# A batched transposed matmul: fixed instruction order, stores on ScalarE's queue, the last four stores held back

## Chip, cores, metric

One core of a Trainium2 chip. The time is the device time of a run in microseconds (us); the span is the time from the first to the last instruction of the profiled run, some 1.8 us shorter. A run of one core has no second die to compare with, so a run counts as fast when it lies within 1.5% of the fastest of its kernel; ratios and profiles below are of fast runs. Batches are numbered 0 to 15.

## The reference

```python
# a: (16, 512, 512) = batch, k, m      b: (16, 512, 512) = batch, n, k      both float32
def reference(a, b):
    return np.matmul(a.transpose(0, 2, 1), b.transpose(0, 2, 1)).astype(np.float32)
```

Each batch reads 1 MB of a and 1 MB of b and writes 1 MB: 48 transfers of 1 MB in all.

## The kernel before

Per batch, VectorE casts b to bf16 (`bc`), TensorE transposes it (eight 128x128 blocks, two bf16 in each float32), VectorE copies the transposes to SBUF, ScalarE casts a, TensorE does sixteen matmuls into four PSUM tiles, and ScalarE and VectorE evict two of these each.

```python
LAG = 3
def load(i):                       # b_sb, a_sb: 4 buffers each
    nc.sync.dma_start(b_sb, b_v[i]);  nc.sync.dma_start(a_sb, a_v[i])

def prepare(i):
    nc.vector.tensor_copy(bc, b_sb)
    for j in range(KJ):
        for no in range(NO):
            nc.tensor.transpose(bt_ps[:, no, :], bc_w[:, no, j, :], identity)
        nc.vector.tensor_copy(bt_w[:, j, :, :], ...)        # cut
    for h in range(2):
        nc.scalar.copy(a_bf[...], a_sb[...])                # cut

def multiply(i):
    for rm in range(MO):           # four matmuls into o_ps, then
        if rm % 2 == 0: nc.scalar.copy(o_sb[:, rm, :], o_ps)
        else:           nc.vector.tensor_copy(o_sb[:, rm, :], o_ps)

for i in range(B + 1):             # the scheduler may reorder this
    if i < B:          load(i); prepare(i)
    if i >= 1:         multiply(i - 1)
    if i >= LAG + 1:   nc.sync.dma_start(out_v[i - 1 - LAG], o_tiles.pop(i - 1 - LAG))
for j in range(B - LAG, B):        # last three stores
    nc.sync.dma_start(out_v[j], o_tiles.pop(j))
```

Of the kernel before, what the change touches and what calls it, by code (L numbers as in the profile page):

```python
# [1 line left out]

# [5 lines left out]


@with_exitstack
def kernel(
    ctx: ExitStack,
    tc: tile.TileContext,
    a: bass.AP,
    b: bass.AP,
    out: bass.AP,
):
    nc = tc.nc
    P = 128  # L20
    B, K, M = a.shape
    _, N, _ = b.shape
    KO = K // P
    KJ = KO // 2
    MO = M // P
    NO = N // P

    f32 = mybir.dt.float32
    cdt = mybir.dt.bfloat16



    a_v = a.rearrange("b (ki ko) m -> b ki ko m", ko=KO)
    b_v = b.rearrange("b (ni no) k -> b ni no k", no=NO)
    out_v = out.rearrange("b (mi mo) n -> b mi mo n", mo=MO)

    const = ctx.enter_context(tc.tile_pool(name="const", bufs=1))
    identity = const.tile([P, P], f32)
    make_identity(nc, identity)

    a_pool = ctx.enter_context(tc.tile_pool(name="a_pool", bufs=4))
    b_pool = ctx.enter_context(tc.tile_pool(name="b_pool", bufs=4))
    ac_pool = ctx.enter_context(tc.tile_pool(name="ac_pool", bufs=3))
    bc_pool = ctx.enter_context(tc.tile_pool(name="bc_pool", bufs=2))
    bt_pool = ctx.enter_context(tc.tile_pool(name="bt_pool", bufs=3))
    o_pool = ctx.enter_context(tc.tile_pool(name="o_pool", bufs=6))
    psum_t = ctx.enter_context(tc.tile_pool(name="psum_t", bufs=4, space=bass.MemoryType.PSUM))
    psum_o = ctx.enter_context(tc.tile_pool(name="psum_o", bufs=4, space=bass.MemoryType.PSUM))

    LAG = 3  # L50
    o_tiles, a_tiles, b_tiles, a_use, b_use = {}, {}, {}, {}, {}

    def load(i):
        b_tiles[i] = b_sb = b_pool.tile([P, NO, K], f32, name="b_sb")
        nc.sync.dma_start(b_sb, b_v[i])  # L55
        a_tiles[i] = a_sb = a_pool.tile([P, KO, M], f32, name="a_sb")
        nc.sync.dma_start(a_sb, a_v[i])  # L57

    def prepare(i):
        b_sb, a_sb = b_tiles.pop(i), a_tiles.pop(i)  # L60



        bc = bc_pool.tile([P, NO, K], cdt, name="bc")
        nc.vector.tensor_copy(bc, b_sb)  # L65
        bc_w = bc.bitcast(f32).rearrange("p no (pk j) -> p no j pk", j=KJ)
        bt_sb = bt_pool.tile([P, KJ, N], f32, name="bt_sb")


        bt_w = bt_sb.rearrange("p j (ni no) -> p j ni no", no=NO)  # L70
        for j in range(KJ):
            bt_ps = psum_t.tile([P, NO, P], f32, name="bt_ps")
            for no in range(NO):
                nc.tensor.transpose(bt_ps[:, no, :], bc_w[:, no, j, :], identity)  # L74
            nc.vector.tensor_copy(bt_w[:, j, :, :], bt_ps.rearrange("p no ni -> p ni no"))  # L75
        b_use[i] = bt_sb.bitcast(cdt).rearrange("p j (n h) -> p j h n", h=2)

        a_bf = ac_pool.tile([P, KO, M], cdt, name="a_bf")
        for h in range(2):
            nc.scalar.copy(a_bf[:, 2 * h:2 * h + 2, :], a_sb[:, 2 * h:2 * h + 2, :])  # L80
        a_use[i] = a_bf.rearrange("p rk (pm rm) -> p rk rm pm", rm=MO)

    def multiply(i):
        a_br, bt_h = a_use.pop(i), b_use.pop(i)
        o_tiles[i] = o_sb = o_pool.tile([P, MO, N], f32, name="o_sb")
        for rm in range(MO):
            o_ps = psum_o.tile([P, N], f32, name="o_ps")
            for rk in range(KO):
                nc.tensor.matmul(  # L89
                    o_ps,  # L90
                    a_br[:, rk, rm, :],
                    bt_h[:, rk // 2, rk % 2, :],
                    start=(rk == 0),
                    stop=(rk == KO - 1),
                )
            if rm % 2 == 0:
                nc.scalar.copy(o_sb[:, rm, :], o_ps)  # L97
            else:
                nc.vector.tensor_copy(o_sb[:, rm, :], o_ps)  # L99



    for i in range(B + 1):
        if i < B:
            load(i)
            prepare(i)
        if i >= 1:
            multiply(i - 1)
        if i >= LAG + 1:
            nc.sync.dma_start(out_v[i - 1 - LAG], o_tiles.pop(i - 1 - LAG))  # L110
    for j in range(B - LAG, B):
        nc.sync.dma_start(out_v[j], o_tiles.pop(j))


# [1 line left out]
_INS = ['a', 'b']  # L116
_OUTS = [((16, 512, 512), 'float32')]


# [23 lines left out]
```

## Time and profile before

| | before |
|---|---|
| median of the first four runs | 128.36 us (127.01 to 128.58) |
| span of the profiled run | 125.4 us |
| DMA engines busy with the kernel's own transfers | 96% of the span |
| TensorE matmul, VectorE, ScalarE busy | 68%, 49%, 41% |

The prediction below reads the rest of this page. The one part that it doesn't show matters later: the list of DMA issues, whose last column is the median time from issue to landing, in us.

```profile
b_sb<-in_b_dram SPq DMA_DIRECT2D x16, 1024.0 KB, 19.6
a_sb<-in_a_dram SPq DMA_DIRECT2D x16, 1024.0 KB, 19.6
out_dram<-o_sb SPq DMA_DIRECT2D x16, 1024.0 KB, 19.6
```

All 48 transfers stand in one queue, so a store waits its turn behind the loads issued before it: 19.6 us is eight transfers of 2.46 us (1 MB at the 427 GB/s of the full slices).

### The profile page before, as it was taken

To read this page: it belongs to the slowest core of one execution; us is meant where nothing else is said; L and a number is where in the kernel's file an instruction comes from. 1 tells how busy PE (TensorE), PEld (TensorE's weight loads), DVE (VectorE), ACT (ScalarE), POOL (GpSimd) and SP (SyncE) were. 2 spreads that over 40 slices of the span, in tenths; PEclk is the share of its full clock that TensorE was granted. 3 is DMA by queue.
4 is the path that set the end of the run, shared out by engine and by line. 5 is a ranking of instruction groups with operands and counts; after the bars stand their busy time and mean duration, and the time that the engine had idled before them with its cause. 6 is when DMAs were issued, how large, how long until landed. Compare 5 with 4: busy or idle time off the path is not lost.

```text
span 125.4 us, 1110 instructions
## 1 busy us (share of the span) xinstructions
PE 85.0 (68%) x384; PEld 45.8 (36%) x384; DVE 60.9 (49%) x80; ACT 51.3 (41%) x65; POOL 0.7 (1%) x6
## 2 busy tenths in 40 slices
PE   0069799999637939396694874939489395693920
PEld 0055356655232334152431534424153152433400
DVE  0255758686452274646607447254742546627420
ACT  4044556846305361533618063361701708154210
POOL 2000000000000000000000000000000000000000
PEclk9999999999995899999859999999976999999996
DMA  3999999999999999999999999999999999999835
GB/s 94 426 431 423 426 423 426 418 350 421 413 428 431 423 426 426 434 428 421 423 431 431 423 415 428 434 423 418 426 436 423 423 423 431 428 418 426 371 154 219
DMA packets 6918, 50.41 MB, mean 402 GB/s; under 512 B 768, under 2 KB 768, under 8 KB 768
## 3 DMA queue, kind: packets, MB, share of 16 engines
q1 hardware_dynamic: 6912, 50.33, 96.1%
q8 instruction: 3, 0.05, 0.2%
q14 instruction: 3, 0.02, 0.0%
HBM read 33.55 MB, written 16.78 MB: 401 GB/s over the span
## 4 chain that ended last, share of the span: by engine, by line
PE 47%; DMA 22%; DVE 17%; issue 7%; ACT 2%; SPq 1%; ACTq 0%
PE o_ps L89 41%; DMA a_sb<-in_a_dram 22%; DVE bc L65 10%; PE bt_ps L74 7%; DVE bt_sb L75 6%; ACT a_bf L80 2%; DVE o_sb L99 1%; SPq L55 1%; SPq L110 0%; ACTq L80 0%; SPq L57 0%
## 5 line engine op out<-in xcount | busy, mean ns | idle before, releaser
L89 PE MATMUL o_ps<-bt_sb,a_bf 128*128 128x512 bf16 x256 | 66.7, 414 | 5.1 <-DVE bt_sb L75 3.0
L89 PEld LDWEIGHTS <-a_bf 128*128 128x128 bf16 x256 | 29.6, 117 | 38.1 <-issue 12.5
L99 DVE COPY o_sb<-o_ps 128x512 f32<-128x512 f32 x32 | 22.1, 691 | 37.8 <-PE o_ps L89 17.0
L97 ACT COPY o_sb<-o_ps 128x512 f32<-128x512 f32 x32 | 18.8, 587 | 52.6 <-PE o_ps L89 52.6
L74 PE MATMUL bt_ps<-identity,bc 128*128 128x128 f32 x128 | 19.6, 298 | 29.9 <-DVE bc L65 29.9
L80 ACT CAST a_bf<-a_sb 128x1024 bf16<-128x1024 f32 x32 | 31.9, 1045 | 15.0 <-DMA a_sb<-in_a_dram 14.7
L74 PEld LDWEIGHTS bt_ps<-identity,bc 128*128 128x128 f32 x128 | 17.4, 209 | 35.6 <-issue 35.0
L75 DVE COPY bt_sb<-bt_ps 128x512 f32<-128x512 f32 x32 | 20.7, 686 | 14.6 <-PE bt_ps L74 14.6
L65 DVE CAST bc<-b_sb 128x2048 bf16<-128x2048 f32 x16 | 19.5, 1220 | 7.4 <-DMA b_sb<-in_b_dram 7.4
L80 ACT ACT_TABLE_LOAD x1 | 1.3, 1283 | 0.7 <-PEq L127 0.7
masks.py:199 POOL TENSOR_SCALAR_AFFINE_SELECT identity<-identity 128x128 f32<-128x128 f32 x1 | 0.3, 295 | 0.1
masks.py:197 POOL MEMSET identity<- 128x128 f32 x1 | 0.2, 205 | 0.3 <-POOLq L127 0.3
L127 POOL MEMSET const-bfloat16-1.0<- 128x1 bf16 x1 | 0.1, 102 | 0.0
L127 POOL MEMSET const-uint8-127<- 128x1 uint8 x1 | 0.1, 102 | 0.0
L127 POOL MEMSET const-float32-0.0<- 128x1 f32 x1 | 0.1, 99 | 0.2 <-issue 0.2
L127 POOL MEMSET const-float32-1.0<- 128x1 f32 x1 | 0.1, 99 | 0.0
## 6 DMA issues: line engine op xcount, KB each, us to landing
b_sb<-in_b_dram SPq DMA_DIRECT2D x16, 1024.0 KB, 19.6
a_sb<-in_a_dram SPq DMA_DIRECT2D x16, 1024.0 KB, 19.6
out_dram<-o_sb SPq DMA_DIRECT2D x16, 1024.0 KB, 19.6
```

The source lines that it names most:

```text
L55: nc.sync.dma_start(b_sb, b_v[i])
L65: nc.vector.tensor_copy(bc, b_sb)
L74: nc.tensor.transpose(bt_ps[:, no, :], bc_w[:, no, j, :], identity)
L75: nc.vector.tensor_copy(bt_w[:, j, :, :], bt_ps.rearrange("p no ni -> p ni no"))
L80: nc.scalar.copy(a_bf[:, 2 * h:2 * h + 2, :], a_sb[:, 2 * h:2 * h + 2, :])
L89: nc.tensor.matmul(o_ps, a_br[:, rk, rm, :], bt_h[:, rk // 2, rk % 2, :], start=(rk == 0), stop=(rk == KO - 1),)
L97: nc.scalar.copy(o_sb[:, rm, :], o_ps)
L99: nc.vector.tensor_copy(o_sb[:, rm, :], o_ps)
L127: nc = _bacc.Bacc("TRN2", target_bir_lowering=False, num_devices=1)
```

## The change

Its intent: let no scheduler reorder the engines; transpose b of the next batch ahead of the matmuls of this one; give the stores a queue of their own; and near the end keep the DMA engines for the last loads, so that the four stores held back fill the time of the last batches' compute.

```diff
-    LAG = 3
+    DEPTH = 4
+    HELD = 4
+    def store(i):
+        nc.scalar.dma_start(out_v[i], o_tiles.pop(i))
     # prepare(i) is split into turn_b(i) and cast_a(i); turn_b does all 8 transposes
     # into one tile of two PSUM banks (2 buffers instead of 4), then both copies     (cut)
-    for i in range(B + 1): ...                                                      (cut)
+    with tc.manual_schedule():
+        for i in range(DEPTH):
+            load(i)
+        turn_b(0)
+        cast_a(0)
+        for i in range(B):
+            if i + 1 < B:
+                turn_b(i + 1)
+            multiply(i)
+            if i + 1 < B:
+                cast_a(i + 1)
+            if i < B - HELD:
+                store(i)
+            elif i + 2 >= B:
+                for j in range(B - HELD if i + 2 == B else i, i + 1):
+                    store(j)
+            if i + DEPTH < B:
+                load(i + DEPTH)
```

More of the change, by code (lines that the diff above doesn't have):

```diff
@@ L46 @@
     o_pool = ctx.enter_context(tc.tile_pool(name="o_pool", bufs=6))
-    psum_t = ctx.enter_context(tc.tile_pool(name="psum_t", bufs=4, space=bass.MemoryType.PSUM))
+    psum_t = ctx.enter_context(tc.tile_pool(name="psum_t", bufs=2, space=bass.MemoryType.PSUM))
     psum_o = ctx.enter_context(tc.tile_pool(name="psum_o", bufs=4, space=bass.MemoryType.PSUM))
-    LAG = 3
+    DEPTH = 4
+    HELD = 4
     o_tiles, a_tiles, b_tiles, a_use, b_use = {}, {}, {}, {}, {}
@@ L57, in load, with turn_b @@
         nc.sync.dma_start(a_sb, a_v[i])
-    def prepare(i):
-        b_sb, a_sb = b_tiles.pop(i), a_tiles.pop(i)
+    def store(i):
+        nc.scalar.dma_start(out_v[i], o_tiles.pop(i))
+    def turn_b(i):
+        b_sb = b_tiles.pop(i)
         bc = bc_pool.tile([P, NO, K], cdt, name="bc")
@@ L67, in prepare, with cast_a @@
         bt_sb = bt_pool.tile([P, KJ, N], f32, name="bt_sb")
-        bt_w = bt_sb.rearrange("p j (ni no) -> p j ni no", no=NO)
+        bt_ps = psum_t.tile([P, KJ, NO, P], f32, name="bt_ps")
         for j in range(KJ):
-            bt_ps = psum_t.tile([P, NO, P], f32, name="bt_ps")
             for no in range(NO):
-                nc.tensor.transpose(bt_ps[:, no, :], bc_w[:, no, j, :], identity)
-            nc.vector.tensor_copy(bt_w[:, j, :, :], bt_ps.rearrange("p no ni -> p ni no"))
+                nc.tensor.transpose(bt_ps[:, j, no, :], bc_w[:, no, j, :], identity)
+        for j in range(KJ):
+            nc.vector.tensor_copy(
+                bt_sb[:, j, :].rearrange("p (ni no) -> p ni no", no=NO),
+                bt_ps[:, j, :, :].rearrange("p no ni -> p ni no"),
+            )
         b_use[i] = bt_sb.bitcast(cdt).rearrange("p j (n h) -> p j h n", h=2)
+    def cast_a(i):
+        a_sb = a_tiles.pop(i)
         a_bf = ac_pool.tile([P, KO, M], cdt, name="a_bf")
@@ L99, in multiply @@
                 nc.vector.tensor_copy(o_sb[:, rm, :], o_ps)
-    for i in range(B + 1):
-        if i < B:
+    with tc.manual_schedule():
+        for i in range(DEPTH):
             load(i)
-            prepare(i)
-        if i >= 1:
-            multiply(i - 1)
-        if i >= LAG + 1:
-            nc.sync.dma_start(out_v[i - 1 - LAG], o_tiles.pop(i - 1 - LAG))
-    for j in range(B - LAG, B):
-        nc.sync.dma_start(out_v[j], o_tiles.pop(j))
+        turn_b(0)
[13 more added lines that the diff above has]
+                load(i + DEPTH)
 _INS = ['a', 'b']
```

## The prediction

> **What bounds the kernel now.** I read the page's DMA rows first, because 50.33 MB in 125.4 us leaves little room.
>
> ```profile
> PEclk9999999999995899999859999999976999999996
> DMA  3999999999999999999999999999999999999835
> GB/s 94 426 431 423 426 423 426 418 350 421 413 428 431 423 426 426 434 428 421 423 431 431 423 415 428 434 423 418 426 436 423 423 423 431 428 418 426 371 154 219
> q1 hardware_dynamic: 6912, 50.33, 96.1%
> ```
>
> Each slice is 3.135 us. The middle slices hold about 427 GB/s, so 1 MB (1,048,576 bytes) takes 2.46 us and the 48 transfers need 118 us. The rest of the span is lost in few places: the first slice (2.4 us), the dip in slice 9 (0.6 us), and the last three slices, which miss 56, 273 and 208 GB/s of 427, together 3.9 us. A better order can win part of those 3.9 us and hardly anything else.
>
> Second, the chain of waits in order of time, because a full DMA row doesn't say that the DMA ends last.
>
> ```profile
> 105.41 0.04 DVE o_sb L99
> 105.44 0.57 issue
> 106.02 1.23 DVE bc L65
> 107.24 0.14 issue
> 107.38 0.73 PE bt_ps L74 x4
> ...
> 108.13 0.70 DVE bt_sb L75
> 108.84 0.04 issue
> 108.88 3.81 PE o_ps L89 x16
> ```
>
> From 43 us to the end the chain contains no DMA at all. It is one ring: the last eviction of batch i on VectorE, the cast of b of the next batch behind it, transposes, their copy, sixteen matmuls. It takes 7.30 us a batch, beside 3 x 2.46 = 7.37 us of DMA. So two bounds lie on top of each other, and the ring decides when the last output exists. The timeline shows the ring's gaps on TensorE:
>
> ```profile
> 107.38 1.20 PE L74 MATMUL bt_ps<-identity,bc 128*128 128x128 f32 x8 [2.01 <-DVE bc L65]
> 108.88 3.79 PE L89 MATMUL o_ps<-bt_sb,a_bf 128*128 128x512 bf16 x16 [0.30 <-DVE bt_sb L75]
> 111.80 0.59 ACT L97 COPY o_sb<-o_ps 128x512 f32<-128x512 f32 x1 [0.55 <-PE o_ps L89]
> 112.28 2.00 ACT L80 CAST a_bf<-a_sb 128x1024 bf16<-128x1024 f32 x2
> ```
>
> 2.01 + 1.20 + 0.30 + 3.79 = 7.30. The last matmuls start at 116.18 and end at 119.98; the last store is issued at 120.76 and takes 3.9 us to land (the shortest landing of the output's DMAs), which gives 124.7 and the span of 125.4 with 0.7 us after it. The last loads were issued at 89.02 and 91.54 and took about 19.6 us, so they were in by 109 and 111: the last batch waited for the ring, not for its data.
>
> **What the Trainium skill says.** "DMA: Bandwidth & Descriptors", section "Issuing engines are not separate DMA queues": transfers started by different engines run on the same 16 DMA engines; only issue time is saved. The trace agrees as far as it goes: 427 GB/s come from one queue with all engines full, so a second queue has nothing to add. The same page, "Queues, rings and completion order", says that an engine serves the queue rows with work in turn, packet by packet. So stores on ScalarE's queue would pass the waiting loads at half the rate, without changing the sum; only one queue is used before, so this isn't shown. "TensorE: Matmul & The Clock Gate", its table at the top, calls ScalarE and VectorE strict FIFO. The trace agrees: each cast of b starts 0.61 us after the eviction ahead of it, at 106.02 after 105.41, though its data is long in. The same page's Part 1 gives half clock after an idle window of about 3.4 us. Here the clock falls with gaps of 3.5 us between the real matmuls (three times, batch 61.87 takes 5.38 us instead of 3.79), so 1.6 us each.
>
> **The change part by part.**
>
> Order. The new text puts turn_b(i+1) ahead of multiply(i) and, with the order fixed, so do the engines. On VectorE: cast b(i+1), two copies, two evictions of batch i, cast b(i+2). On TensorE: transposes(i+1), matmuls(i), transposes(i+2). The copies now lie under matmuls, so the 0.30 goes. But cast b(i+2) still stands behind the last eviction of batch i, so the 2.01 stays, and the 1.20 stays. The ring is 2.01 + 1.20 + 3.79 = 7.00 us, a gain of 0.30 a batch or 4.5 us in 15. ScalarE's ring (eviction, two casts of 1.0 us) is shorter and doesn't count.
>
> Start. Batch 0's matmuls started at 9.19 before; now they wait for the transposes of batch 1. Its b landed at 10.58; cast 1.23, gap 0.14, transposes at half clock 1.96 (as the first ones were): 13.9. Sixteen matmuls, the first four of them at half clock (0.43 against 0.237 us, my guess of the count): 18.5. Then batch i's matmuls start at 18.5 + 2.01 + 1.20 + 7.00 (i-1), batch 14's at 112.7. The start gives back what the ring wins.
>
> Do the loads keep up? In flight or queued are at most the four loads of each input, as before; each batch frees 7.37 us of DMA work per 7.00 us, so the DMA never runs dry before the loads end. b of batch 14 has 29 loads and 12 stores up to it: 3.1 + 41 x 2.46 = 104.0, so its matmuls of batch 13 can't start before 106.6, where the ring says 105.7. That costs up to 0.9 us. The last load lands at 3.1 + 44 x 2.46 = 111.3, as early as before. I take batch 14 at 113.6, and with a mean of a bit over half a clock drop (below) 114.5.
>
> Hold. Stores 12 to 14 stand on ScalarE behind its last eviction of batch 14 and the casts of a(15). From the start of batch 14's matmuls: third group 2.92 (116.18 to 119.10 before), eviction 0.48, casts 2.00: issued at +5.4, so 119.9. Between 111.3 and about 120.5 the DMA has nothing to do: 9 us, where the kernel before lost 3.9. Batch 15's matmuls start after the first half of the cast, +4.5, end at +8.3, its last store is issued at +9.1, while the three ahead occupy the DMA until +13.5, so it queues. End: 5.4 + 0.1 + 1.44 (landing 3.9 less 2.46) + 4 x 2.46 + 0.7 = 17.5 after 114.5, a span of 132.0. The run of the profile took 127.22 for a span of 125.4, so 1.8 on top: **133.8 us**.
>
> In short: ring -4.5, later start and colder clock +4.4, DMA limit +0.9, and after the last matmuls 3 more stores than before. From the end of batch 15's matmuls to the end of the span it is now 17.5 - 8.3 = 9.2 us instead of 5.4: +3.8. The rest is clock drops and the ScalarE cast that delays batch 15.
>
> **Rivals.**
>
> First, the intent: the holding clears the way for the last loads, and four stores fill the DMA while the last batches compute. Then there would be 118 us of transfers, 3.1 ahead and 1.5 behind: a span near 122.6, some 124.4 us. For it speaks the DMA row. Against it: the loads aren't what the last batches wait for, and the stores wait for ScalarE's work after the loads, not only for the loads.
>
> Second, the hold costs, but the DMA idles less: if the early ring ran as fast as batches 1 to 4 do before (4.85 us apart, where the cast of b stood ahead of the evictions), batch 14 would be bound by its load at 111.1 and the end be 128.6, or 130.4 us. The fixed order forbids that on VectorE.
>
> Third, the clock. The gap between real matmuls falls from 3.50 to 3.21 us. If only gaps over the window drop the clock, no drop is left and the time is about 132.9; if it goes on as before, two or three drops make 136 to 138.
>
> Fourth, loads and stores interleaved by packet could move less than 427 GB/s; 2% less would be 2 us more, which adds to a ring that waits for loads.
>
> **Range and chances.** The centre is 133.8, 4% above the median of 128.47 and 5% above the profiled run's 127.22. Downward the ring sets a floor: 112.7 without drops and waits gives 132.0, and a warmer start or one cast fewer on the path gives some 130.5. Upward two more drops and a slower DMA give 137.5. Faster by over 2% needs the first rival: 4%. Within 2% (125.9 to 131.0) needs the second, or a start warmer than I think: 9%. Slower: 87%.
>
> **What would show it.** A DMA row with two to three nearly empty slices after 111 us, then full slices to the end; TensorE's wait for the cast of b still 2.0 us a batch but no wait for the copy; matmul starts 7.0 us apart; the three stores issued on ScalarE's queue right behind the last casts near 120; the last load landed near 111. I am wrong if the last casts on ScalarE end before 113, if the DMA row stays full to the end, or if the ring is shorter than 6.7 us.

## The result

| | before | after |
|---|---|---|
| median | 128.36 us | 132.19 us (131.66 to 134.0, the last a slow run) |
| ratio | | 1.0308 (95% interval 1.0207 to 1.0408) |
| span of the profiled run | 125.4 us | 130.8 us |
| mean granted clock | 0.951 | 0.961 |

Slower by 3.1%. A ratio is the mean time of one kernel's fast runs over that of the other's of the same rounds, so not quite the ratio of the medians.

The page of the changed kernel, the rows in 40 slices of 3.27 us (clock, DMA, GB/s), then the two DMA queues (q1 SyncE's, q10 ScalarE's) and the stores' time to landing:

```profile
PEclk9999999999999995999999999977999999999995
DMA  3999999999999999999999999999999999104995
GB/s 125 426 424 434 419 426 328 408 426 426 431 418 429 429 426 426 429 426 429 426 426 431 424 429 424 419 431 421 426 431 424 426 434 419 58 5 200 431 411 241
q1 hardware_dynamic: 4608, 33.56, 61.6%
q10 hardware_dynamic: 2304, 16.78, 30.6%
...
out_dram<-o_sb ACTq DMA_DIRECT2D x16, 1024.0 KB, 9.0
```

Three slices near the end (58, 5 and 200 GB/s) miss 369, 422 and 227 of 427, together 7.8 us of empty DMA. And a store now lands 9.0 us after its issue instead of 19.6: it passes loads that were issued earlier (store 0, issued at 18.78 us, landed at 28.85; b of batch 5, issued at 15.56, at 36.04).

The end in the timeline (start, duration, engine; in brackets the idle time before and what ended it):

```profile
114.44 1.19 PE L75 MATMUL bt_ps<-identity,bc 128*128 128x128 f32 x8 [2.01 <-DVE bc L69]
115.47 3.79 PE L98 MATMUL o_ps<-bt_sb,a_bf 128*128 128x512 bf16 x15
...
118.39 0.58 ACT L106 COPY o_sb<-o_ps 128x512 f32<-128x512 f32 x1 [1.23 <-PE o_ps L98]
118.57 0.34 ACTq L61 DMA_DIRECT2D out_dram<-o_sb  x1
118.87 1.05 ACT L89 CAST a_bf<-a_sb 128x1024 bf16<-128x1024 f32 x1
119.03 0.37 ACTq L61 DMA_DIRECT2D out_dram<-o_sb  x1
...
119.97 0.64 PE L98 MATMUL o_ps<-bt_sb,a_bf 128*128 128x512 bf16 x2 [0.71 <-ACT a_bf L89]
120.07 0.34 ACTq L61 DMA_DIRECT2D out_dram<-o_sb  x1
120.91 2.88 PEld L98 LDWEIGHTS <-a_bf 128*128 128x128 bf16 x14 [0.80 <-ACT a_bf L89]
...
125.09 0.34 ACTq L61 DMA_DIRECT2D out_dram<-o_sb  x1
```

The ring is there (2.01 us of waiting for the cast of b, no wait for the copy) and takes 6.84 us (107.59, the transposes before, to 114.44). The held stores go out at 118.57, 119.03 and 120.07. The first is issued 0.3 us before the first of the two casts ahead of it in ScalarE's program begins.

In the middle two matmul groups run at half clock, and two transposes wait much longer than the ring's 2.01 us (3.44 and 2.84). TensorE's timeline:

```profile
47.39 1.19 PE L75 MATMUL bt_ps<-identity,bc 128*128 128x128 f32 x8 [2.07 <-DVE bc L69]
48.42 5.40 PE L98 MATMUL o_ps<-bt_sb,a_bf 128*128 128x512 bf16 x15
...
77.78 1.20 PE L75 MATMUL bt_ps<-identity,bc 128*128 128x128 f32 x8 [3.44 <-DVE bc L69]
78.81 3.80 PE L98 MATMUL o_ps<-bt_sb,a_bf 128*128 128x512 bf16 x16
85.45 1.27 PE L75 MATMUL bt_ps<-identity,bc 128*128 128x128 f32 x8 [2.84 <-DVE bc L69]
86.94 4.95 PE L98 MATMUL o_ps<-bt_sb,a_bf 128*128 128x512 bf16 x15 [0.23 <-issue]
```

### The profile page after: what moved, and what is told of

The parts are those of the page before. It is cut to its first block, busy times and chain, and to the rows that moved or that the text cites. A ratio compares the mean times of both kernels' runs of the same rounds, so it can differ in the third digit from the quotient of the medians.

```text
span 130.8 us, 1093 instructions
## 1 busy us (share of the span) xinstructions
PE 82.2 (63%) x377; PEld 46.0 (35%) x384; DVE 61.3 (47%) x80; ACT 50.4 (39%) x65; POOL 0.7 (1%) x6
## 4 chain that ended last, share of the span: by engine, by line
PE 45%; DMA 29%; DVE 12%; issue 6%; ACT 2%; SPq 1%; ACTq 1%; DVEq 0%
PE o_ps L98 34%; DMA b_sb<-in_b_dram 22%; PE bt_ps L75 11%; DVE bc L69 10%; DMA out_dram<-o_sb 7%; ACT a_bf L89 2%; DVE o_sb L108 1%; ACTq L61 1%; ACT o_sb L106 0%; SPq L58 0%; SPq L56 0%; DVEq L69 0%
## 5 line engine op out<-in xcount | busy, mean ns | idle before, releaser
L98 PE MATMUL o_ps<-bt_sb,a_bf 128*128 128x512 bf16 x249 | 63.7, 405 | 1.6 <-ACT a_bf L89 1.0
L75 PE MATMUL bt_ps<-identity,bc 128*128 128x128 f32 x128 | 20.8, 310 | 40.5 <-DVE bc L69 40.5
```

Source lines behind the costliest of these rows:

```text
L75: nc.tensor.transpose(bt_ps[:, j, no, :], bc_w[:, no, j, :], identity)
L98: nc.tensor.matmul(o_ps, a_br[:, rk, rm, :], bt_h[:, rk // 2, rk % 2, :], start=(rk == 0), stop=(rk == KO - 1),)
```

## The experiments

First theories. A: the ring ends late and the hold adds little. B: the hold is the main cost, as the prediction's +3.8 us says. Medians, with the kernel before of the same job:

| run | what differs | median us | before us | ratio (95%) |
|---|---|---|---|---|
| no_hold | nothing held | 132.32 | 128.49 | 1.0312 (1.024 to 1.039) |
| stores_sp | all stores on SyncE's queue | 130.02 | 128.49 | 1.0123 (1.006 to 1.019) |
| tail_sp | last four stores on SyncE's queue | 132.76 | 128.49 | 1.0310 (1.022 to 1.040) |
| cast_early | next cast of b ahead of the evictions | 131.04 | 128.49 | 1.0220 (1.013 to 1.031) |
| order_alone | the order only; stores SyncE, 3 behind | 127.13 | 128.06 | 0.9963 (0.992 to 1.000) |
| before_stores_act | before, stores on ScalarE's queue | 130.38 | 128.06 | 1.0249 (1.017 to 1.033) |
| own_early | transposes(i) before matmuls(i) | 131.78 | 128.06 | 1.0314 (1.020 to 1.043) |
| own_early_sp | own_early, stores SyncE | 127.45 | 128.06 | 0.9952 (0.992 to 0.999) |
| order_lag_act | order_alone, stores on ScalarE's queue | 132.72 | 128.25 | 1.0355 (1.030 to 1.041) |
| order_nolag | order_alone, stores not behind | 128.71 | 128.25 | 1.0037 (0.999 to 1.009) |
| own_early_lag | own_early_sp, stores 3 behind | 126.46 | 128.25 | 0.9865 (0.982 to 0.991) |
| lag_act_tail_sp | order_lag_act, late stores SyncE | 126.94 | 127.67 | 0.9948 (0.992 to 0.997) |

All gave correct results. Measured against a line of 2%, no_hold, tail_sp and order_lag_act are slower than before, cast_early, before_stores_act and own_early unclear, and the rest the same. The medians of stores_sp and own_early include one slow run, that of own_early_sp two; the ratios don't.

**no_hold**

```diff
-    HELD = 4
+    HELD = 0
```

> The changed kernel with no store held: every store is issued behind the casts of its turn, order and queues as in the change. Theory A (the ring of VectorE and TensorE ends late, the hold only adds a little): the last store was issued at 125.1 and needs 3.9 us to land plus 0.7 us to the end, so the span goes from 130.8 to about 129.7 and the time to about 131.1 us, still slower than before by some 2%. Theory B (the hold is the main cost, as the prediction's 3.8 us has it): about 128.4 us, level with before.

Measured 132.32 us: neither. Dropping the hold returned nothing (1.0312 against 1.0308), so B falls as it stood. But the 1.1 us that A hoped for didn't come either: without the hold, the last load landed at 115.7 us instead of 113.5, since store 12 (issued at 106.63 us, landed at 115.39) passed it.

**stores_sp**

```diff
-        nc.scalar.dma_start(out_v[i], o_tiles.pop(i))
+        nc.sync.dma_start(out_v[i], o_tiles.pop(i))
```

> The changed kernel with all stores on SyncE's queue, same places in the text, same hold. Theory A (the queue is not the cause): within 1 us of the changed kernel, 131.5 to 133.5 us; loads are issued a little later since they stand behind the store on one sequencer. Rival (stores on ScalarE's queue delay its evictions or pass the loads, and that costs): 1.5 us or more faster, below 130.7 us.

Measured 130.02 us, 2.2 us below the changed kernel: A missed, and the queue is suspect. (On SyncE's program the hold is none: no cast or eviction stands ahead of the stores, and store 12 went out at 103.8 us.)

**tail_sp**

```diff
-            if i < B - HELD: ...                            (cut: the hold)
             if i + DEPTH < B:
                 load(i + DEPTH)
+            (nc.scalar if i < B - HELD else nc.sync).dma_start(out_v[i], o_tiles.pop(i))
```

> The changed kernel with the last four stores on SyncE's queue behind the last load instead of held on ScalarE, so that the DMA engines get stores 12 to 14 as soon as they exist. Theory A: the empty DMA slices after 110 us partly fill, but the last store is still issued near 125, so about 131.1 us, like no_hold. Theory B: about 128.4 us.

132.76 us, both wrong: freeing the last four stores from ScalarE does nothing while the first twelve are still there.

**cast_early**: `turn_b` split, so that on VectorE the cast of b of batch i+2 precedes the evictions of batch i.

```diff
             if i + 1 < B:
                 turn_b(i + 1)          # now without the cast
+            if i + 2 < B:
+                cast_b(i + 2)
             multiply(i)
```

> The changed kernel with one thing moved: on VectorE the cast of b of batch i+2 stands ahead of the two evictions of batch i instead of behind them; queues and hold unchanged. Theory A: the 2.0 us wait of TensorE per batch goes away, the transfers set the pace, the last load still lands near 111, batch 14 starts near 111 instead of 115.5, the stores held are issued near 114.5, and the span is about 126 us, the time about 128 us, level with before. Theory B (the hold costs whatever the ring does): 131 us or more.

131.04 us: A missed by 3 us, level with what B says. The ring was gone (after batch 0 the next three transposes followed without a wait), but then TensorE waited for loads: the last b landed at 110.9 us, batch 14 started at 113.97 and ran its first matmuls at half clock (granted clock of the run 0.906), and the held stores went out at 118.10. So taking the ring away doesn't win the time back: VectorE now waits for b 15 times, 45.4 us in all, where the changed kernel waits 4 times, 8.0 us. The clock is a rival that this run doesn't part from the loads: five stretches at half clock before the end, against two in the changed kernel.

Two new theories. C: two multiplies instead of one follow the last b's transposes. D: ScalarE's queue lets stores pass loads.

**order_alone**

```diff
-        nc.scalar.dma_start(out_v[i], o_tiles.pop(i))
+        nc.sync.dma_start(out_v[i], o_tiles.pop(i))
...
-            if i < B - HELD: ...                            (cut: the hold)
             if i + DEPTH < B:
                 load(i + DEPTH)
+            if i >= 3:
+                store(i - 3)
+        for j in range(B - 3, B):
+            store(j)
```

> The change's fixed order alone: every engine in the order of the new text, but the stores on SyncE's queue three batches behind as before, none held. Theory C (two multiplies instead of one come after the transposes of the last b, some 4.5 us, and that is the main cost): 129.5 to 131 us, still slower than before. Rival D (stores on ScalarE's queue overtake the loads and are the main cost): level with before, 127.5 to 129.

127.13 us, a little below before: C falls. D stands, though this run takes away the queue, the missing lag and the hold at once. With the same order and other stores the loss is gone, so what the change does with the stores costs all of it. Its clock and DMA rows:

```profile
PEclk9999999999999999999999999999999999999995
DMA  3999999999999999999999999999999999999945
GB/s 86 434 431 424 421 424 424 424 426 421 426 421 413 403 429 429 429 405 418 421 431 426 424 426 403 429 426 424 421 434 426 426 421 421 437 429 413 382 170 212
```

Full to slice 38, and no half clock between batch 0 and the last slice (before has three such stretches, so the 0.4% is the order and the clock together). Who waited for b, first the changed kernel, then order_alone (total us, times, longest):

```profile
DVE bc L69 <- DMA b_sb<-in_b_dram: 8.0, 4, 5.6
```

```profile
DVE bc L69 <- DMA b_sb<-in_b_dram: 5.9, 2, 5.6
```

The two waits of the start are in both. The changed kernel has two more, 2.1 us, at 76 and 84 us. The two profiles can be set against each other by batch 14's matmuls, which start at 115.47 and at 110.51. From transposes to transposes the changed kernel has 1.43 + 0.83 us more where b was late and 1.60 + 1.61 us more at half clock, and its start was 0.61 us quicker: 4.86 of the 4.96 us. After that its end takes 0.5 us longer (15.3 against 14.8 us).

"As before" in the expectation is not what ran. Before's text keeps its stores three batches behind, but the scheduler moved them forward: in its trace store 0 is issued at 15.51 us, 0.06 us after the last eviction of its batch, and no store is issued more than 8.1 us after it. In order_alone stores 0 to 8 do wait 15.0 us. So the lag is new in order_alone, and before has none to lose.

**before_stores_act**

```diff
-            nc.sync.dma_start(out_v[...], ...)              (both places)
+            nc.scalar.dma_start(out_v[...], ...)
```

> The kernel before with nothing changed but the queue: its stores go out on ScalarE's queue, three batches behind, order left to the scheduler. Theory C: within 1.3 us of before, 127.5 to 129.8 us. Rival D: 130.5 us or more.

130.38 us, 2.5% slower than before: outside C's range (up to 129.8) and just short of D's (130.5 or more). But it is not a test of the queue alone. With the queue changed in the text, the scheduler chose another order: on VectorE the cast of the next b now stands between the two evictions of a batch (cast at 54.87 us, eviction at 56.01), where before it stands behind both from batch 5 on (evictions at 49.56 and 51.09 us, cast at 51.70). And the clock is lower (0.886 to 0.910 in its runs, 0.941 to 0.956 in the fast ones of before). The cast's wait for b, before and in this run:

```profile
DVE bc L65 <- DMA b_sb<-in_b_dram: 7.4, 4, 5.6
```

```profile
DVE bc L65 <- DMA b_sb<-in_b_dram: 44.6, 15, 5.6
```

A cast that stands earlier also waits longer for the same b, as in cast_early (45.4 us, 15 times), so this difference is not the queue's alone either.

**own_early**: transposes of batch i directly ahead of matmuls of batch i; on VectorE the cast of b of batch i+1 ahead of the evictions of batch i. Stores and hold as in the change.

```diff
         for i in range(B):
-            if i + 1 < B:
-                turn_b(i + 1)
+            turn_b(i)                  # without the cast
+            if i + 1 < B:
+                cast_b(i + 1)
+            cast_a(i)
             multiply(i)
-            if i + 1 < B:
-                cast_a(i + 1)
```

> The change with its fixed order replaced: the transposes of batch i directly ahead of the multiply of batch i, so one multiply is left after the last b, and on VectorE the cast of b of batch i+1 ahead of the evictions of batch i, so that this order has no long ring; stores on ScalarE and the hold as in the change. Theory C: the last b lands near 111, cast, transposes, copies and one multiply end near 118, the held stores are issued near 112.5, span 124 to 125.5 us, time 125.8 to 127.3 us, faster than before by 1 to 2%. If the extra multiply is not the cause it stays like cast_early, 130 to 131 us.

131.78 us, 4.5 us above C's range. Its chain of waits (start, duration, what) shows another way in which a store on ScalarE hurts:

```profile
99.06 0.70 DVE o_sb L111
99.76 0.03 ACTq L61
99.79 0.04 issue
99.83 0.34 ACTq L61
...
100.27 0.89 issue
101.16 1.05 ACT a_bf L92
102.21 0.05 issue
102.25 3.37 PE o_ps L101 x14
```

The store on ScalarE waits for VectorE's last eviction, and the cast of a that the next matmuls need stands behind the store in ScalarE's program. That is a ring of its own, 6.61 us a turn (94.55 to 101.16, the same cast one batch apart).

**own_early_sp**: own_early with the edit of stores_sp.

> own_early with all stores on SyncE's queue. Theory C alone: as own_early within 1 us. Rival D (or a part of it): 1.5 to 2 us faster than own_early, as stores_sp was against the changed kernel.

127.45 us, 4.3 us below own_early: more than D foresaw, presumably since the ring on ScalarE goes too.

Theory E then put it down to the loads' lead alone: stores three batches behind should help on either queue.

**order_lag_act**: order_alone with `nc.scalar` in `store`.

> order_alone with one thing changed: its stores, three batches behind, go out on ScalarE's queue. Theory E (what costs is that stores are transferred while loads are still wanted, so that loads land after the ring asks for them; ScalarE's queue makes it worse because a store lands 9 us after its issue instead of 16 to 20): three batches of lag still leave the loads ahead, the last b lands near 104 and the ring asks for it at 108, so 127 to 128.7 us, within 1.5 us of order_alone. Rival (issuing on ScalarE costs in itself, wherever the loads are): 129.5 us or more.

132.72 us: E missed by 4 us. But the reason isn't its rival's either. The last b landed at 103.5 us, and batch 14's matmuls started at 110.67, as in order_alone (110.51); TensorE never waited for a late b. The loss is all at the end:

```profile
DMA  4999999999999999999999999999999967074995
GB/s 120 410 433 433 415 433 418 423 425 418 423 423 380 423 423 423 428 428 428 425 425 433 420 425 420 425 428 425 428 428 425 425 265 285 15 305 200 435 405 240
```

```profile
106.87 0.34 ACTq L61 DMA_DIRECT2D out_dram<-o_sb  x1
113.70 0.34 ACTq L61 DMA_DIRECT2D out_dram<-o_sb  x1
118.71 3.15 ACTq L61 DMA_DIRECT2D out_dram<-o_sb  x4
```

Store i-3 stands in ScalarE's program behind the evictions of batch i, so it can't go before them, though its data is three batches old. The DMA engines begin to run dry at 106 us, and four stores (9.8 us) are left after the last multiply. In order_alone the same lines on SyncE ran ahead once the last load was issued (stores 8 to 12 at 89.0, 89.5, 91.6, 94.6 and 101.4 us; from store 11 on within 0.1 us of the batch's last eviction, but for the last).

**order_nolag**: order_alone with `store(i)` in its own turn.

> order_alone with one thing changed: each store is issued in its own turn on SyncE's queue instead of three batches later. Theory E: the loads lose their lead of three stores (7.4 us), the last b lands near 110 to 111 instead of 101.4, TensorE waits again for b, 129.3 to 130.7 us, like stores_sp. Rival (the lag does nothing, only the queue counts): 127.1 us as order_alone.

128.71 us: the direction of E (1.0037 against 0.9963), but only 1.6 us (128.71 against 127.13), where at least 2.2 were expected. TensorE waited for b about 0.5 us more than the ring's 2.01 at 103.7 and at 111.1 us. The lag matters a little (the two intervals still overlap, and the runs are of two jobs), less than ScalarE does. order_nolag issues its loads and stores in the same order as before did, which fits its 1.0037.

**own_early_lag**: own_early_sp with order_alone's store lines (load first, store three behind).

> The best of the parts together: own_early's order on VectorE and TensorE, stores on SyncE's queue three batches behind, none held. With the loads ahead and no long ring the compute ends early and the 48 transfers alone set the time: 3.1 + 48 x 2.46 us = 121.2 and about 1.5 us behind, a span of 122 to 123.5 us, 123.8 to 125.3 us, 2.5 to 3.5% faster than before. If the loads fall behind all the same: 127 us as own_early_sp.

126.46 us, 1.3% faster than before and the fastest median of the study, though 1.2 us short of what was expected. The DMA row is full to the last slice but one:

```profile
DMA  3999999999999999999999999999999999999981
GB/s 92 424 432 429 427 421 421 421 421 421 421 413 421 421 427 419 424 424 429 429 421 427 413 421 424 424 432 429 427 427 424 432 413 427 432 427 427 424 366 47
```

The last store landed at 123.6 us: 48 transfers in 120.5 us, 2.51 us each. With this the transfers alone set the time.

**lag_act_tail_sp**: the last question was whether a store on ScalarE's queue costs by being there, or by where it makes the transfer fall.

```diff
-            if i >= 3:
-                store(i - 3)
-        for j in range(B - 3, B):
-            store(j)
+            if 3 <= i < 12:
+                store(i - 3)                                  # ScalarE's queue
+            elif i >= 12:
+                for j in range(9 if i == 12 else i, i + 1):
+                    nc.sync.dma_start(out_v[j], o_tiles.pop(j))
```

> order_lag_act with one thing changed: stores 0 to 8 stay on ScalarE's queue three batches behind, and stores 9 to 15, which come after the last load is issued, go out on SyncE's queue, which has no other work by then. Theory F (ScalarE's queue costs nothing in itself; it costs where a store is transferred, either ahead of loads that are wanted, or, held in ScalarE's program behind later evictions, too late, so that the DMA stands empty): compute as in order_alone, its last multiply ends near 119.5, no empty DMA slices before that, span 125.3 to 126.3 us, 126.9 to 128.3 us. Rival (stores on ScalarE's queue cost by being there): 129.5 us or more.

126.94 us: F holds (span 124.5 us, even 0.8 below its range). Nine of sixteen stores go over ScalarE's queue and cost nothing (0.9948 against order_alone's 0.9963). They come three batches late, and no store is left behind ScalarE's last evictions:

```profile
DMA  4999999999999999999999999999999999999954
GB/s 84 421 429 440 429 421 421 421 424 421 421 421 416 405 421 426 432 429 426 432 421 421 426 429 426 419 429 424 421 429 426 432 424 429 426 424 421 424 216 184
```

Landing times, worked out from the trace as issue plus time to landing of each transfer and so good to 0.1 us, put the cases side by side:

| | b of batch 10 landed | stores landed by then | last b | last load | ratio |
|---|---|---|---|---|---|
| before | 71.8 us | 6 | 108.6 | 111.1 | 1 |
| after | 76.3 us | 7 | 111.1 | 113.5 | 1.0308 |
| no_hold | 74.0 us | 7 | 111.2 | 115.7 | 1.0312 |
| order_nolag | 72.5 us | 6 | 109.6 | 112.0 | 1.0037 |
| order_alone | 64.2 us | 3 | 101.4 | 103.8 | 0.9963 |
| order_lag_act | 65.0 us | 3 | 103.5 | 108.0 | 1.0355 |
| lag_act_tail_sp | 65.7 us | 3 | 103.2 | 105.6 | 0.9948 |

What the queue does is thus this. The DMA engines move 427 GB/s whichever queue feeds them, so a store done early is a load done late, by 2.46 us each. On SyncE's one queue a store that really goes out three batches behind lands when the loads have a lead, and SyncE's program, which has no compute, issues it as soon as its data is there. On ScalarE it either goes at once and overtakes loads that the ring needs (after, no_hold, tail_sp), or it is put later in the program and then waits for work that it has nothing to do with (order_lag_act: evictions of later batches).

In the changed kernel's trace 2.3 us of the cost are waits for b and 3.2 us are matmuls at half clock, and no run parts the two. The half clock alone isn't it: the changed kernel's two other fast runs have a granted clock of 0.976 and 0.972 instead of 0.961, which I estimate to be one stretch at half clock fewer, and they took 131.66 and 131.83 us instead of 132.56, still 3 us above before.

## Why the prediction was right, and where it wasn't

The time (133.8 us, measured 132.19) and the direction are right. The stretch without transfers at the end came as described; its sizes, and which part of the change is to blame, are wrong. That the number came so close is partly luck. Up to batch 14, late loads and half clock took 5.5 us where the prediction gave them 1.8; a shorter start and ring, 2.7 us, hid most of that, and an end 2.2 us shorter than predicted hid the rest.

- **Order and ring.** Predicted 7.00 us a batch with the 2.01 us wait kept and the copy's 0.30 hidden; measured 6.84. The first matmul starts 1.03 us after the transposes' start, not 1.20. "The start gives back what the ring wins": order_alone has the sum, 0.4% faster than before, but without the three half-clock stretches of before (1.6 us each), so it is no clean test. Right in its sizes.
- **Start.** Matmuls of batch 0 predicted at 13.9, ending at 18.5; measured 13.62 and 17.96. Right.
- **DMA limit.** This is the first mis-sized term. "That costs up to 0.9 us" became 2.3 us of waiting for b. The 12 stores assumed ahead of the last loads were the right number but not the whole matter. The stores took their turns from 20 us on, so the lead was gone by batch 9, not by batch 13. The prediction had the means, since it cited that the queues are served in turn, but it used them for the sum only, not for who comes first. The last load, predicted at 111.3, landed at 113.5.
- **Clock.** "A bit over half a clock drop" of 1.6 us became two, 3.2 us in the profiled run. One follows a late b. The other, at 48.42 us, follows a wait of only 2.07 us. In the trace's clock record all changes lie on a grid of 3.41 us, and the two drops begin at 48.90 and 86.45 us. In every second stretch of that grid from 18.18 us on, the matmuls into o_ps fill 0.59, 0.57, 0.56 and 0.54 us, and the clock stays full. In the next one, 45.49 to 48.90 us, they fill 0.48 us, and it falls. What is missing there, 0.06 us, is a late load: b of batch 6 landed at 45.93 us, and its cast began at 46.02, 0.66 us after the start of the eviction ahead of it instead of 0.60 to 0.61. In before's trace the clock falls after stretches with 0, 0.11 and 0.20 us and stays after 0.50. So this drop too may hang on a late load, by a hair; that is a reading of two traces and not a rule, for in own_early_lag the clock fell after a stretch with 1.6 us. The prediction's own reading, drops with gaps of 3.5 us "three times", doesn't hold: one of the three follows a gap of 5.0 us, and eight gaps of 3.5 us had no drop.
- **Hold.** "Issued at +5.4" was +3.10 (118.57 after 115.47), and the span ended 15.3 us after the start of batch 14's matmuls instead of 17.5. The prediction let the stores wait for the casts ahead of them in ScalarE's program. They wait only until these are handed on. The Trainium skill has it, in "Perfetto Trace Analysis", section "DVE / Act Engine Instruction": once an instruction is pushed into the wait queue, the sequencer is ready for the next. The trace agrees: the store at 118.57, the first cast ahead of it at 118.87, the second at 119.81. The empty stretch was still 7.8 us (9 predicted).
- **The blame.** "After the last matmuls 3 more stores than before: +3.8" is the step that failed. From the end of batch 15's matmuls (124.29) to the end of the span it was 6.5 us against 5.4, so +1.1, and taking the hold away returned nothing. The late loads and the slow clock took its place: batch 14 started at 115.47, 1.0 us later than predicted although the ring was shorter. The two errors of opposite sign left the sum 1.2 us too high in the span.
- **The rivals.** The first (a full DMA row to the end) is what order_alone and own_early_lag look like, and they get there without a hold or ScalarE's queue. The fourth, fewer GB/s from mixing queues, is refuted: from slice 9 to slice 34 the changed kernel moves 426 GB/s on average (418 to 434), before 425 from slice 10 to slice 37.

Open: what decides the clock drops in general; why the DMA row of the changed kernel dips to 328 GB/s in slice 7; and whether order_nolag is really 0.9% better than stores_sp (their intervals overlap). In stores_sp each load stands behind a store in SyncE's program (b of batch 4 is issued at 19.55 us instead of 6.95), which is likely the reason, but it was not tried alone.

## What to carry to other kernels

When the DMA engines are full, a second queue adds no bandwidth; it only decides which transfer comes first, so ask of each store which load it pushes back. Keep stores a few iterations behind the loads, and issue them from an engine whose program has nothing else to wait for: on ScalarE here a store could not go out before what stood ahead of it in the program was handed to the engine, and what stood behind it waited for the store. The hold returned nothing here, kept or taken away; whether one that is released before the DMA engines run dry would pay, no run shows.

## What the Trainium skill lacked or had wrong

- "DMA: Bandwidth & Descriptors", section "Issuing engines are not separate DMA queues", says that issuing from several engines only saves sequencer time. For bandwidth the runs agree (427 GB/s with one queue or two). For time it is too little: issued from ScalarE instead of SyncE, the same lines took the kernel from 0.9963 to 1.0355 of before (order_alone, order_lag_act), and a store's median time to landing from 14.7 to 8.9 us.
- The same page's "Queues, rings and completion order" describes the turns between queues, but doesn't draw out that a store on the second queue overtakes loads that were issued earlier (9.0 us to landing instead of 19.6), and I found no page that draws out what the wait of a DMA does to the program of an engine that computes: in own_early the wait of a store for VectorE, with the cast of a behind it, made a ring of 6.61 us.
- "TensorE: Matmul & The Clock Gate", Part 1, ties the half clock to an idle window of about 3.4 us. It doesn't say how idle. In the changed kernel the clock fell after a stretch of 3.41 us in which o_ps matmuls filled 0.48 us and transposes 1.19 us, and stayed after one with 0.54 and 1.19 us; order_alone went through fourteen waits of 2.01 us with transposes behind them at full clock, with 1.17 us of matmuls or more in each stretch.
